# Seven products instead of eight in two FFNs, with three of the four sums of weights made by accumulating transfers

## The chip, the core and the metric

The kernel runs on one core of a Trainium2 chip. The metric is the device time of one execution in microseconds, as the median of several runs. The core's engines are TensorE (PE in the profile, with its weight loads as PEld), VectorE (DVE), ScalarE (ACT), GpSimd (POOL) and SyncE (SP); the last two issue transfers here, which 16 DMA engines carry out. Each engine works off its own instructions strictly in order, and so do the queues on which SyncE and GpSimd issue transfers: an instruction that waits holds up all that stand behind it.

## The reference

One block over 256 tokens of width 2048, all in float32. The change touches the two feed-forward networks (FFNs), whose hidden width is 5632:

```python
def swiglu_ffn(x, w_gate, w_up, w_down):
    return (jax.nn.silu(x @ w_gate) * (x @ w_up)) @ w_down
...
x = x + 0.5 * swiglu_ffn(rmsnorm(x, norm_ffn1_g[l]), ffn1_w_gate[l], ffn1_w_up[l], ffn1_w_down[l])
h = rmsnorm(x, norm_mix_g[l])
proj = h @ w_in[l]
... # attention in chunks and retention, each with its own output projection, merged by gates
x = x + merged @ w_out[l]
x = x + 0.5 * swiglu_ffn(rmsnorm(x, norm_ffn2_g[l]), ffn2_w_gate[l], ffn2_w_up[l], ffn2_w_down[l])
return rmsnorm(x, norm_final_g)
```

Gate and up are matrices of 2048 x 5632, down is one of 5632 x 2048. Between the two FFNs stand the mixers: an input projection 2048 x 11264 (`w_in`) and three output projections.

## The kernel before

**Steps.** All weights are streamed once, in blocks of 256 rows by 512 columns (512 KB, `KC` = 2 slices of 128 rows). One such block is a step, and the program is 768 steps in a row, 264 in each FFN and 240 in the mixers. A step loads its block on SyncE's queue into one of 4 raw buffers (L94; `raw` with a number in the rows). ScalarE then copies it to the reduced float32 type that TensorE reads at full rate (`hi`, L107), and VectorE subtracts that from the raw block to get what is left (`lo`, L108). There are 5 pairs of hi and lo buffers. I call this pair of operations a split. It is done a few steps ahead of use (`split_upto`), as far as the buffers go.

**Products.** The activations are split in the same way, once, when they are transposed. Each product is made of three, hi by hi, hi by lo and lo by hi (L125 to L127). The 256 tokens are two tiles of 128, so that a step has 2 slices x 2 token tiles x 3 = 12 matmuls of 128x128 by 128x512, with the weights moving. They add into two PSUM banks, one for each token tile (`acc`); there are four of those, and four more for transposes and the like (`side`).

**FFN.** The hidden columns are cut into 11 blocks of 512. A block has 8 steps of gate, after which ScalarE evicts the two banks with SiLU (L374), and 8 of up, after which VectorE multiplies (L379). Two steps later the product is transposed (L269) and split, as an operand of the down projection. Down runs in two halves, after blocks 0 to 5 and after blocks 6 to 10, and each half adds to the residual in SBUF (`xall`), with 4 x 12 or 4 x 10 steps. The norm's gain is put on in the transposes of the input (`put`, L322), its scale for each token at the evictions.

**Order.** A scheduler does not decide anything: the order on each engine is that of the program, with `later(n, fn)` to put work n steps on. At the start, loads of weights and the four column quarters of x are issued by turns (`load_x`, L173). The mixers use two tables of 512 KB each, which GpSimd's queue loads (`decay`, L201, and `biasT`, the bias read from the spread-out table `rel_ext`). The last `TAIL` = 4 steps are done token tile by token tile, so that the first one's finish overlaps the second one's products.

## Time and profile before

| what | value |
|---|---|
| median of 3 runs | 2179.64 us (2179.56 to 2180.44) |
| the profiled execution, its time and its span | 2180.46 us, 2178.4 us |
| TensorE clock granted, mean | 0.999 |
| busy: PE, PEld, DVE, ACT, POOL | 2167.7, 1802.5, 1121.6, 963.0, 21.6 us |
| moved by DMA | 414.51 MB, 190 GB/s in the mean |
| share of the 16 DMA engines taken by SyncE's queue (q1) | 57.9% |
| the chain that ended last | PE 99% |

The span goes from the first instruction to the last, and the time of an execution holds a little more than its span. In the rows below, a row of the waits or of the groups names engine, operation, output and inputs and line. In rows of the chain and of the timeline the first number is the time since the start of the span and the second the time until the last of the row's instructions ended, both in us; x4 is the number of instructions in the row; what stands in brackets is an idle time before it and what ended it. Rows of transfers give the size and the us from issue to landing. Busy time of an engine is an average over the whole span; what a wait costs is seen only at its own place.

### The profile page before, as it was taken

To read this page: it belongs to the slowest core of one execution; us is meant where nothing else is said; L and a number is where in the kernel's file an instruction comes from. 1 tells how busy PE (TensorE), PEld (TensorE's weight loads), DVE (VectorE), ACT (ScalarE), POOL (GpSimd) and SP (SyncE) were. 2 spreads that over 40 slices of the span, in tenths; PEclk is the share of its full clock that TensorE was granted. 3 is DMA by queue.
4 is the path that set the end of the run, shared out by engine and by line. 5 is a ranking of instruction groups with operands and counts; after the bars stand their busy time and mean duration, and the time that the engine had idled before them with its cause. 6 is when DMAs were issued, how large, how long until landed. Compare 5 with 4: busy or idle time off the path is not lost.

```text
span 2178.4 us, 25308 instructions
## 1 busy us (share of the span) xinstructions
PE 2167.7 (100%) x9865; PEld 1802.5 (83%) x9865; DVE 1121.6 (51%) x1192; ACT 963.0 (44%) x1104; POOL 21.6 (1%) x36
## 2 busy tenths in 40 slices
PE   9999999999999999999999999999999999999998
PEld 7888888888888888888888888888888888888887
DVE  5544554445545544556655555554544544444554
ACT  6444433444444444454444444454444433444443
POOL 0000000000000000000000000000000000000000
PEclk9999999999999999999999999999999999999999
DMA  7655655666665555555555555556656556666554
GB/s 253 208 188 187 222 192 194 212 188 190 187 209 184 184 190 187 175 163 178 167 177 190 188 192 192 185 183 194 193 184 193 189 194 212 189 192 191 186 192 137
DMA packets 213512, 414.51 MB, mean 190 GB/s; under 512 B 12864, under 2 KB 13616, under 8 KB 213392
## 3 DMA queue, kind: packets, MB, share of 16 engines
q1 hardware_dynamic: 211424, 406.90, 57.9%
q0 software_dynamic: 1824, 5.93, 0.9%
q8 instruction: 77, 1.26, 0.2%
q14 instruction: 43, 0.35, 0.0%
q10 hardware_dynamic: 144, 0.07, 0.0%
HBM read 409.17 MB, written 3.67 MB: 190 GB/s over the span
## 4 chain that ended last, share of the span: by engine, by line
PE 99%; issue 0%; DMA 0%; ACT 0%; DVE 0%; POOL 0%; POOLq 0%; ACTq 0%
PE acc L125 32%; PE acc L126 32%; PE acc L127 32%; PE f2a0p L269 0%; PE f1a0p L269 0%; PE n1p L322 0%; DMA grows<-in_norm_ffn_g_dram 0%; PE f2a6p L269 0%; PE f1a6p L269 0%; PE mgp L269 0%; PE nmp L322 0%; PE n2p L322 0%; PE as L479 0%; PE rs L537 0%; PE av L514 0%
## 5 line engine op out<-in xcount | busy, mean ns | idle before, releaser
L108 DVE TENSOR_TENSOR lo<-raw,hi 128x1024 fp32r<-128x1024 f32 (+1 forms) x769 | 938.8, 1223 | 1014.0 <-ACT hi L107 1013.6
L107 ACT CAST hi<-raw 128x1024 fp32r<-128x1024 f32 (+1 forms) x769 | 808.2, 1052 | 1106.8 <-PE acc L127 1081.8
L125 PE MATMUL acc<-hi,nmh 128*128 128x512 f32 x704 | 277.8, 395 | 0.0
L125 PE MATMUL acc<-hi,n1h 128*128 128x512 f32 x704 | 276.2, 392 | 0.0
L125 PE MATMUL acc<-hi,n2h 128*128 128x512 f32 x704 | 274.8, 390 | 0.0
L126 PE MATMUL acc<-lo,n1h 128*128 128x512 f32 x704 | 274.7, 390 | 0.0
L127 PE MATMUL acc<-hi,n1l 128*128 128x512 f32 x704 | 274.6, 390 | 0.0
L127 PE MATMUL acc<-hi,nml 128*128 128x512 f32 x704 | 274.5, 390 | 0.0
L126 PE MATMUL acc<-lo,nmh 128*128 128x512 f32 x704 | 274.1, 389 | 0.0
L127 PE MATMUL acc<-hi,n2l 128*128 128x512 f32 x704 | 274.0, 389 | 0.0
L126 PE MATMUL acc<-lo,n2h 128*128 128x512 f32 x704 | 273.9, 389 | 0.0
L127 PEld LDWEIGHTS acc<-hi,n1l 128*128 128x128 f32 x704 | 132.4, 188 | 27.6
L127 PEld LDWEIGHTS acc<-hi,nml 128*128 128x128 f32 x704 | 132.2, 188 | 27.9
L125 PEld LDWEIGHTS acc<-hi,n1h 128*128 128x128 f32 x704 | 132.6, 188 | 27.3
L126 PEld LDWEIGHTS acc<-lo,n1h 128*128 128x128 f32 x704 | 132.4, 188 | 27.3 <-DVE lo L108 0.4
L127 PEld LDWEIGHTS acc<-hi,n2l 128*128 128x128 f32 x704 | 132.2, 188 | 27.5
L126 PEld LDWEIGHTS acc<-lo,n2h 128*128 128x128 f32 x704 | 132.2, 188 | 27.1
L125 PEld LDWEIGHTS acc<-hi,n2h 128*128 128x128 f32 x704 | 132.2, 188 | 27.0
L126 PEld LDWEIGHTS acc<-lo,nmh 128*128 128x128 f32 x704 | 132.3, 188 | 26.2
L125 PEld LDWEIGHTS acc<-hi,nmh 128*128 128x128 f32 x704 | 132.3, 188 | 26.2
L125 PE MATMUL acc<-hi,f2a0h 128*128 128x512 f32 x192 | 74.8, 390 | 0.0
L125 PE MATMUL acc<-hi,f1a0h 128*128 128x512 f32 x192 | 74.8, 389 | 0.0
(266 smaller groups left out, 2107.3 us busy)
## 6 DMA issues: line engine op xcount, KB each, us to landing
raw<-in_ffn_w_up_dram SPq DMA_DIRECT2D x176, 512.0 KB, 3.5
raw<-in_ffn_w_down_dram SPq DMA_DIRECT2D x176, 512.0 KB, 3.6
raw<-in_w_in_dram SPq DMA_DIRECT2D x176, 512.0 KB, 3.5
raw<-in_ffn_w_gate_dram SPq DMA_DIRECT2D x175, 512.0 KB, 3.5
raw<-in_w_out_dram SPq DMA_DIRECT2D x32, 512.0 KB, 3.7
raw<-in_w_out_att_dram SPq DMA_DIRECT2D x16, 512.0 KB, 4.3
raw<-in_w_out_ret_dram SPq DMA_DIRECT2D x16, 512.0 KB, 4.3
xall<-in_x_dram SPq DMA_DIRECT2D x3, 512.0 KB, 7.5
```

The source lines that it names most:

```text
L107: nc.scalar.copy(hi[:, p, :], raw[:, p, :])
L108: nc.vector.tensor_sub(lo[:, p, :], raw[:, p, :], hi[:, p, :].bitcast(F32))
L125: nc.tensor.matmul(acc, ahi[:, ts], whi[:, cs], start=first, stop=False)
L126: nc.tensor.matmul(acc, ahi[:, ts], wlo[:, cs], start=False, stop=False)
L127: nc.tensor.matmul(acc, alo[:, ts], whi[:, cs], start=False, stop=last)
```

## The change

In each FFN, blocks 1 to 10 compute gate and up together; block 0 and all the down steps stay as they were. Take the activations X (256 tokens by 2048) as 2 x 2 parts: token halves 1 and 2 by two halves of the inner dimension, which alternate by four slices of 128. Take the weights of one block as 2 x 2 parts: the same two inner halves (top and bottom) by gate and up. Eight products of such parts give the result; the program now forms it from seven (a form of Strassen's scheme, due to Winograd), with sums of activations, sums of weights and sums of results.

The four sums of activations (s5, s7, s6, s3) are made once for each of the two FFN norms, by VectorE (`add_up`), and split like the rest. Four sums of weights are made for each block, 4 tiles of 512 KB each. Two sets of tiles stay in SBUF over the block: k, which begins as the top of gate, and x, which begins as the top of up.

- T1: x = x + k, an accumulating transfer from SBUF to SBUF on GpSimd's queue, issued when x's load is issued (`load_second`, L478 in the rows)
- T2: x = x + bottom of up, the same kind, up to 3 steps ahead of its use (`early`)
- T3: k = x - k, on VectorE (L517)
- T4: x = x + bottom of gate, an accumulating transfer again (L519)

So a block pair (I call it a group; there are 20) has these steps, each with a tile number 0 to 3:

| step | splits | products, bank |
|---|---|---|
| p0 to p3 (phase 0) | k, x (after T1) | X11 by k in a; s5 by x in c |
| q0 to q3 (phase 1) | bottom of up (raw), x (after T2) | s6 by x in a; s3 by raw in c |
| r0 to r3 (phase 2) | bottom of gate (raw), k (after T3) | s7 by k in a; X12 by raw in b |
| s0 to s3 (phase 3) | x (after T4) | X22 by x in a |

A step p, q or r has two splits and 12 matmuls (two products over one token half each), a step s has one split and 6. After each phase banks are evicted (`end`): after p3 ScalarE copies a and c; after q3 it copies a, and VectorE adds c to that; after r3 VectorE adds a and b to earlier results; after s3 ScalarE evicts a. SiLU and the multiplication follow as the parts come ready.

The group's steps are woven with 8 standard steps, D1 to D8, mostly of down, in this order: p0 p1 p2 p3 D1, q0 q1 D2 q2 q3 D3, r0 D4 r1 D5 r2 D6 r3 D7, s0 s1 s2 s3 D8 (`WOVEN`; the last group of an FFN has more of them). Down is no longer done in halves, but for each pair of blocks. The hi and lo buffers go from 5 pairs to 4, raw buffers stay at 4, 8 tiles (`KEPT`) hold k and x. A step is prepared only when as many split buffers are free as it needs, and while a step is prepared the transfers that have a buffer free are issued. In numbers of instructions: 9156 matmuls of 512 columns become 8724, 120 of 256 columns become 24; 769 casts become 1009; GpSimd issues 240 transfers more; SyncE issues 782 before and after.

```diff
-SPLIT_BUFS = 5
-ACT_TILES = 26
-TAIL = 4
+SPLIT_BUFS = 4
+KEPT = 8
+ACT_TILES = 30
+TAIL = 2
 AHEAD = (2, 3)
+BY_DMA = ("T1", "T2", "T4")
+HALF_K = D // P // 2
+LEAD = 8
+EARLY = 3
+WOVEN = "ppppD" "ppDppD" "pDpDpDpD" "ssssD"
+WOVEN_LAST = "pDppDpD" "pDpDpDpD" "pDpDpDpD" "ssDssD"
...
+    def load_some():
+        while state["dma"] < len(transfers):
+            ring, fn = transfers[state["dma"]]
+            if not room[ring]:
+                return
+            room[ring] -= 1
+            fn()
+            state["dma"] += 1
+
+    def prep_upto(n, c):
+
+        while state["prep"] < min(len(steps), n):
+            s = steps[state["prep"]]
+            if s.slots > state["slots"]:
+                return
+            load_some()
+            for e in steps[state["prep"] : state["prep"] + EARLY]:
+                if e.early is not None and e.early():
+                    e.early = None
+            state["slots"] -= s.slots
+            s.prep()
+            for ring in s.frees:
+                room[ring] += 1
+            state["prep"] += 1
+            load_some()
...
+        def add_up(self, p, n):
+
+            if n == 0:
+                self.f = [act_tile(F32, f"{self.name}f{p}{i}") for i in range(2)]
+                self.f = [f.rearrange("p a (h q) -> p h a q", h=2)[:, i] for f in self.f for i in range(2)]
+                x0, x1 = self.raw.pop(2 * p), self.raw.pop(2 * p + 1)
+                a11, a21, a12, a22 = [x[:, :, t * P : (t + 1) * P] for x in (x0, x1) for t in range(NT)]
+                s5, s7, s6, s3 = self.f
+                nc.vector.tensor_sub(s5, a22, a21)
+                nc.vector.tensor_sub(s7, a11, a21)
+                nc.vector.scalar_tensor_tensor(s6, s5, -1.0, a11, op0=ALU.mult, op1=ALU.subtract)
+                nc.vector.scalar_tensor_tensor(s3, s6, -1.0, a12, op0=ALU.mult, op1=ALU.subtract)
+            for i in (2 * n, 2 * n + 1):
+                self.split_to(self.SUMS[i], slice(4 * p, 4 * p + 4), self.f[i])
...
+            def load_second():
+                self.x[jc] = kept_tile("x")
+                fetch(self.x[jc], self.w[1], self.rows(0, jc), self.col[1])
+                if "T1" in BY_DMA:
+                    nc.gpsimd.dma_start(self.x[jc], self.kept[jc], accum_op=ALU.add)
+
+            def load_raw():
+                made["raw"] = weights_tile(f"raw{name}")
+                i = 2 - phase
+                fetch(made["raw"], self.w[i], self.rows(1, jc), self.col[i])
+
+            def early():
+
+                if "raw" not in made:
+                    return False
+                nc.gpsimd.dma_start(self.x[jc], made["raw"], accum_op=ALU.add)
+                return True
+
+            def two(first, second):
+
+                tiles = []
+                for i, raw in enumerate((first, second)):
+                    hi = wpool.tile([P, KC, NB], F32R, tag="hi", bufs=SPLIT_BUFS, name=f"hi{name}{i}")
+                    lo = wpool.tile([P, KC, NB], F32R, tag="lo", bufs=SPLIT_BUFS, name=f"lo{name}{i}")
+                    nc.scalar.copy(hi, raw)
+                    tiles.append((raw, hi, lo))
+                for raw, hi, lo in tiles:
+                    nc.vector.tensor_sub(lo, raw, hi.bitcast(F32))
+                return [(hi, lo) for _, hi, lo in tiles]
+
+            def prep():
+                x = self.x[jc]
+                if phase == 0:
+                    if "T1" not in BY_DMA:
+                        nc.vector.tensor_add(x, x, self.kept[jc])
+                    made["w"] = two(self.kept[jc], x)
+                elif phase == 1:
+                    raw = made["raw"]
+                    if "T2" not in BY_DMA:
+                        nc.vector.tensor_add(x, x, raw)
+                    made["w"] = two(raw, x)
+                elif phase == 2:
+                    raw, k = made.pop("raw"), self.kept.pop(jc)
+                    nc.vector.tensor_sub(k, x, k)
+                    if "T4" in BY_DMA:
+                        nc.gpsimd.dma_start(x, raw, accum_op=ALU.add)
+                    else:
+                        nc.vector.tensor_add(x, x, raw)
+                    made["w"] = two(raw, k)
+                else:
+                    made["w"] = [split(self.x.pop(jc), name)]
+
+            def products():
+                w = made["w"]
+                if phase == 0:
+                    self.product("a", "a00", jc, w[0], True, False)
+                    self.product("c", "s5", jc, w[1], True, False)
+                elif phase == 1:
+                    self.product("a", "s6", jc, w[1], False, False)
+                    self.product("c", "s3", jc, w[0], False, True)
+                elif phase == 2:
+                    self.product("a", "s7", jc, w[1], False, False)
+                    self.product("b", "a01", jc, w[0], True, True)
+                else:
+                    self.product("a", "a11", jc, w[0], False, True)
+                if jc == n - 1:
+                    self.end(phase)
...
+        def end(self, phase):
+
+            norm, acc, copy = self.norm, self.acc, self.copy
+
+            def copied(key, bank, scale):
+                copy[key] = tmp_tile(f"{self.name}{key}", "qk", 4)
+                nc.scalar.activation(copy[key], acc[bank], AF.Copy, scale=scale)
+
+            if phase == 0:
+                copied("s1", "a", norm.scale(0))
+                copied("s5", "c", norm.minus_scale(1))
+            elif phase == 1:
+                copied("s2", "a", norm.minus_scale(0))
+                r = copy["s2"]
+                nc.vector.scalar_tensor_tensor(r, acc["c"], norm.minus_scale(0), r, op0=ALU.mult, op1=ALU.add)
+                self.evict(0, 1, r)
+            elif phase == 2:
+                r = copy["s5"]
+                nc.vector.scalar_tensor_tensor(r, acc["a"], norm.minus_scale(1), r, op0=ALU.mult, op1=ALU.add)
+                self.evict(1, 1, r)
+                r = copy["s1"]
+                nc.vector.scalar_tensor_tensor(r, acc["b"], norm.scale(0), r, op0=ALU.mult, op1=ALU.add)
+                self.evict(0, 0, r)
+            else:
+                self.evict(1, 0, None, acc["a"])
...
+        queue = plain(0)
+        for pair in range((nblocks + 1) // 2):
+            queue += down(pair)
+        queue = [(job, k) for job in queue for k in range(0, job.nk, KC)]
+
+        def next_standard(n):
+            for job, k in queue[:n]:
+                steps.append(standard(job, k))
+            del queue[:n]
+
+        next_standard(LEAD)
+        for b in range(1, nblocks):
+            group = paired(b).steps()
+            for what in WOVEN if b < nblocks - 1 else WOVEN_LAST:
+                if what == "D":
+                    next_standard(1)
+                else:
+                    steps.append(group.pop(0))
+            assert not group
+        next_standard(len(queue))
```

On ScalarE, around the first eviction of a group, before: the casts of three steps, the two evictions of a gate block, and the casts of the next steps.

```order
L107 CAST hi41_978<-raw41_894 128x1024
L107 CAST hi42_996<-raw42_928 128x1024
L107 CAST hi43_1014<-raw43_946 128x1024
L374 ACTIVATE f1g20_1032<-acc32_0_876,n1rstd_88 128x512
L374 ACTIVATE f1g21_1034<-acc32_1_877,n1rstd_88 128x512
L107 CAST hi44_1036<-raw44_964 128x1024
L107 CAST hi45_1058<-raw45_982 128x1024
```

The same place after the change, the seam of phases 0 and 1 of a group whose first step is number 104 (z104; the two digits behind the name are phase and tile, the last is the first or second split of the step):

```order
L498 CAST hiz104030_2602<-z104k3_2461 128x1024
L498 CAST hiz104031_2605<-z104x3_2479 128x1024
L114 CAST hi108_2623<-raw108_2482 128x1024
L553 ACTIVATE z104s1_2641<-z104a_2567,n1rstd_88 128x512
L553 ACTIVATE z104s5_2643<-z104c_2574,n1minus_89 128x512
L498 CAST hiz104100_2645<-rawz10410_2484 128x1024
L498 CAST hiz104101_2648<-z104x0_2364 128x1024
```

Before, the casts of steps 41 to 43 stood ahead of the evictions after step 39's products; now one cast, that of D1, lies between p3's casts and the evictions, and q0's two come behind them. On VectorE at the seam of phases 1 and 2, after the change (before, the whole program had no such step):

```order
L501 TENSOR_TENSOR loz104131_2737<-z104x3_2479,hiz104131_2736 128x1024
L115 TENSOR_TENSOR lo114_2756<-raw114_2678,hi114_2755 128x1024
L561 SCALAR_TENSOR_TENSOR z104s2_2773<-z104c_2574,n1minus_89,z104s2_2773 128x512
L517 TENSOR_TENSOR z104k0_2362<-z104x0_2364,z104k0_2362 128x1024
L501 TENSOR_TENSOR loz104200_2779<-rawz10420_2697,hiz104200_2778 128x1024
L501 TENSOR_TENSOR loz104201_2782<-z104k0_2362,hiz104201_2781 128x1024
L115 TENSOR_TENSOR lo116_2789<-raw116_2719,hi116_2788 128x1024
```

The sum T3 for r0 (L517) and r0's two subtractions stand behind the addition from bank c, which needs q3's last product. On GpSimd, where the last sums of one group meet the first of the next (z128; before, this queue issued 21 transfers in all, none of them here):

```order
L519 DMA z104x1_2409<-rawz10421_2741 128x1024
L519 DMA z104x2_2454<-rawz10422_2786 128x1024
L478 DMA z128x0_2877<-z128k0_2875 128x1024
L519 DMA z104x3_2479<-rawz10423_2829 128x1024
L478 DMA z128x1_2922<-z128k1_2880 128x1024
L478 DMA z128x2_2967<-z128k2_2945 128x1024
```

The last T4 of the group (into x3, used by s3) now stands behind the first T1 of the next group. On SyncE at the start, before:

```order
L94 DMA raw6_177<-in_ffn1_w_gate_dram 128x2x512
L94 DMA raw7_206<-in_ffn1_w_gate_dram 128x2x512
L173 DMA xall_77<-in_x_dram 128x2x512
L94 DMA raw8_234<-in_ffn1_w_up_dram 128x2x512
L94 DMA raw9_240<-in_ffn1_w_up_dram 128x2x512
```

and after, up to the same loads:

```order
L108 DMA raw7_221<-in_ffn1_w_gate_dram 128x2x512
L108 DMA z8k0_223<-in_ffn1_w_gate_dram 128x2x512
L108 DMA z8x0_225<-in_ffn1_w_up_dram 128x2x512
L108 DMA z8k1_228<-in_ffn1_w_gate_dram 128x2x512
L108 DMA z8x1_230<-in_ffn1_w_up_dram 128x2x512
L108 DMA z8k2_233<-in_ffn1_w_gate_dram 128x2x512
L108 DMA z8x2_235<-in_ffn1_w_up_dram 128x2x512
L108 DMA z8k3_238<-in_ffn1_w_gate_dram 128x2x512
L108 DMA z8x3_240<-in_ffn1_w_up_dram 128x2x512
L219 DMA xall_77<-in_x_dram 128x2x512
L108 DMA raw12_271<-in_ffn1_w_up_dram 128x2x512
```

The eight loads of the first group's k and x, which have buffers from the beginning, now stand ahead of the last quarter of x.

More of the change, by code (lines that the diff above doesn't have):

```diff
@@ L150, in run @@
[L150 removed]
+            steps[c].products()
+            state["slots"] += steps[c].slots
+        prep_upto(len(steps), head)
         state["step"] = head
```

332 lines of the change are left out of this document (212 added, 120 removed).

## The prediction

> **What bounds the kernel now.** I read the page's head first, then the waits of TensorE, then the chain in order of time for the pace of a step.
>
> ```profile
> span 2178.4 us, 25308 instructions
> PE 2167.7 (100%) x9865; PEld 1802.5 (83%) x9865; DVE 1121.6 (51%) x1192; ACT 963.0 (44%) x1104; POOL 21.6 (1%) x36
> ...
> PE gps L184 <- DMA grows<-in_norm_ffn_g_dram: 1.8, 1, 1.8
> PE psw L685 <- POOL mhalf L206: 1.1, 1, 1.1
> ...
> 149.53 0.87 PE f1a0p L269 x8
> 193.94 0.87 PE f1a0p L269 x8
> ```
>
> TensorE is busy in all of the span, and its whole list of waits is 2.9 us. So a matmul less is its time less, as long as nothing new makes TensorE wait. From one set of transposes to the next lie 16 steps of 12 matmuls and 0.87 us of transposes: (193.94 - 149.53 - 0.87) / 192 = 0.2268 us a matmul, 2.72 us a step. One pair of weight blocks with its 8 standard steps ("a group") now costs 24 x 2.72 + 0.9 = 66.2 us.
>
> The other engines have room, and these are their paces when work stands in a row, and the handovers:
>
> ```profile
> 37.69 2.95 ACT L107 CAST hi<-raw 128x1024 fp32r<-128x1024 f32 x3
> 38.77 4.63 DVE L108 TENSOR_TENSOR lo<-raw,hi 128x1024 fp32r<-128x1024 f32 x4 [3.15 <-ACT hi L107]
> ...
> 563.89 1.05 ACT L107 CAST hi<-raw 128x1024 fp32r<-128x1024 f32 x1 [1.67 <-PE acc L127]
> 564.98 1.22 DVE L108 TENSOR_TENSOR lo<-raw,hi 128x1024 fp32r<-128x1024 f32 x1 [1.49 <-ACT hi L107]
> 565.51 0.39 PE L127 MATMUL acc<-hi,n1l 128*128 128x512 f32 x1
> 565.93 1.37 ACT L374 ACTIVATE f1g<-acc,n1rstd 128x512 f32<-128x512 f32 x2 [0.99 <-PE acc L127]
> 567.20 1.04 ACT L107 CAST hi<-raw 128x1024 fp32r<-128x1024 f32 x1
> ...
> L379 DVE SCALAR_TENSOR_TENSOR f1g<-acc,n1rstd,f1g 128x512 f32<-128x512 f32 x22 | 15.4, 743 | 0.0
> ```
>
> A cast takes 1.05 us, and one follows the next after 0.95; a subtraction takes 1.22 and follows after (4.63 - 1.23) / 3 = 1.13; it starts 0.04 after its cast ends (564.98 against 563.89 + 1.05). ScalarE reads a bank 0.42 us after its last matmul began, which is 0.19 after the next may start; two evictions take 567.20 - 565.93 = 1.27, so 0.64 each. An eviction on VectorE costs 15.4 / 22 = 0.70.
>
> **The change, part by part.** *Fewer products.* 20 groups each lose 192 - 168 = 24 matmuls: 480 x 0.2268 = **-108.9 us**, if TensorE goes on without a wait. Transposes stay the same. A group is then 264 x 0.2268 + 0.9 = 60.8 us.
>
> *More splits.* A group has 36 casts instead of 24 and 40 subtractions (36 splits, 4 of the sum left on VectorE). VectorE: 40 x 1.13 + 11 evictions and the like x 0.70 = 53 us of 60.8; ScalarE: 36 x 0.95 + 7 x 0.64 = 39 us. Neither becomes the bound on average, and I cost them nothing there. If the cover were gone, it would show at the seams between the phases, where a split can't be made ahead:
>
> *Seam of phases 0 and 1.* With four split buffers, step q0 is prepared only after p3 is issued, so on ScalarE its casts stand behind the two evictions that wait for p3. From p3's end: second eviction at 0.19, cast of the raw block at 0.83, cast of x 1.78 to 2.83; on VectorE lo of raw from 1.92, lo of x 3.05 to 4.27. TensorE has only D1 (2.72 us) to do, and its second matmul of q0, at 2.95, needs that lo: it waits 1.3 us.
>
> *Seam of phases 1 and 2.* VectorE evicts bank c at 0.19, then makes k (0.89 to 2.11), ScalarE casts k until 3.20, and lo of k ends at 4.46; cover again is one step, D3. Wait 1.5 us. The seam of phases 2 and 3 has D7 and s0 as cover and a chain of about the same length: nothing. Together 2.8 x 20 = **+57 us**; ends 0 (if a split is made earlier than I read) and 4 x 20 = 80 (if VectorE comes late to both).
>
> *The sums by transfer.* 12 a group, 512 KB each, 240 in all. No accumulating transfer is in this trace. The nearest rows are plain transfers of the same size on the same queue, two issued in a row, and what they did to the loads beside them:
>
> ```profile
> L201 POOL DMA_DIRECT2D decay<-in_decay_dram x2: 547/548/549, 616.5 to 617.1; - x2
> ...
> DMA to landing us min/median/max: 6.4/7.1/7.8
> ...
> DMA to landing us min/median/max: 5.6/6.1/6.6
> ...
> raw<-in_ffn_w_down_dram SPq DMA_DIRECT2D x176, 512.0 KB, 3.6
> ...
> raw<-in_ffn_w_down_dram SPq DMA_DIRECT2D x7, 512.0 KB, 4.5
> decay<-in_decay_dram POOLq DMA_DIRECT2D x2, 512.0 KB, 7.1
> ...
> raw<-in_ffn_w_gate_dram SPq DMA_DIRECT2D x4, 512.0 KB, 5.4
> ...
> 10.00:12.00 2.00, 2.00 (x6) 1.52 (x6) 2.00 (x4) 0.74 (x1) 0.00 (x0) 1.00 1.06 404
> ```
>
> The first two rows of landings are decay (6.4 and 7.8) and biasT (5.6 and 6.6). A load lands after 3.6 us alone (median of the run), 4.5 beside the decay pair and 5.4 beside the four of rel_ext. With all engines taken (share 1.06) they move 404 GB/s, so one pass over 512 KB is 1.30 us. The bounds for an accumulating one: 3.6 (a load alone) from below; from above, a second pass for itself and for the one in front of it (2.6), at half the rate where loads share the engines (5.2). I take the same-queue rows and half a second pass, since these are the same queue and shape.
>
> The Trainium skill (DMA: Bandwidth & Descriptors, "Anatomy of one DMA — SWDGE (gpsimd) path") gives 2.0 us plus the bytes at 436 GB/s for a transfer of this queue: 3.2 us for 512 KB. The trace's 5.6 to 7.8 beside loads disagrees; by the skill the two terms below would be nothing and the sum rival A's.
>
> *The last T4 of a group.* It stands on the GpSimd queue behind the first T1 of the next group, and that waits for loads. Clock from the end of r3: s3 starts at 2.72 + 3 x 1.36 = 6.8, its second matmul needs lo at 7.03, so the cast must begin, and T4 have landed, by 7.03 - 1.22 - 0.04 - 1.05 = 4.7. The load of x0 stands on SP's queue behind that of D8, which gets its buffer when lo of D6 ends. k of r2 can be cast when r1 has let its buffer go (-10.88 + 0.19), so lo of k ends at -8.4, lo of D6 at -7.2, later with the standard evictions between; I take -7. An issue on SP costs 0.47 us (row of the start, below). So x0 is issued at -6.1, lands 5.4 later at -0.7, T1 takes 0.55 to issue (decay's row), and T4 starts at -0.1. As decay's second (7.8) it lands at 7.7, 3.0 late; with a full second pass 5.6 late; sharing, 8.2. I take 4.3: **+86 us** for 20 groups, ends 0 and 164. Behind the waiting cast stand D8's and the next group's p0's, so nothing fills the gap.
>
> *T2 of q3.* Its raw block's buffer comes from q0, whose lo of raw ends at 3.14 after p3; load 4.5, T2 6.4: landed at 14.0. q3 starts at 14.9 (q0 to q2 and D2, with the wait above), and x must be cast by 12.9. Late 1.2: **+24 us**, ends 0 and 2.5 x 20 = 50. The other sums have about 1 us or more to spare by the same reckoning.
>
> *The start.*
>
> ```profile
> 3.21 0.47 SPq L173 DMA_DIRECT2D xall<-in_x_dram  x1
> ...
> 10.18 7.18 SPq L94 DMA_DIRECT2D raw<-in_ffn_w_gate_dram  x4
> 17.40 0.46 SPq L173 DMA_DIRECT2D xall<-in_x_dram  x1
> ...
> xall<-in_x_dram SPq DMA_DIRECT2D x1, 512.0 KB, 5.5
> ...
> 22.66 0.58 PEld L322 LDWEIGHTS n1p<-id_sb,xall 128*128 128x128 f32 x4
> ```
>
> The last quarter of x is issued at 17.40, lands at 22.9 and is used as it lands. Now eight loads of k and x go ahead of it: 3.8 us of issuing to 10.4 us of data (8 x 1.30). I take **+8.5**. The sums of activations, once a norm, fall where VectorE is half idle: 0.
>
> *The end.* TAIL goes from 4 to 2, so the second half's last products follow the first half's 2.7 us sooner, and its finish queues behind the first's: **+1.5** (0 to 2.6).
>
> **Sum**: 2178.4 - 108.9 + 57 + 86 + 24 + 8.5 + 1.5 = 2246.5 us of span. The profiled execution took 2180.46 for its 2178.4, 0.8 above the median of the three runs, so 1.2 goes on top: **2248 us**, 3% slower.
>
> **Rivals.** *A: the sums are ready in time, and it is faster.* If the last T4 lands within 4.8 us of issue, only the seams remain: 2178.4 - 108.9 + 57 + 8.5 + 1.5 + 1.2 = 2138 us. For it: the data goes from SBUF to SBUF, and 3.6 us is what a load takes. Against: the rows of that queue. It decides at a lateness of (108.9 - 57 - 10) / 20 = 2.1 us a group: below that the kernel gains. *B: the DMA engines become the bound*, because a sum reads two operands: a group then needs 24 x 1.30 + 12 x 2.60 = 62.4 us of all 16 engines at their best, with 63.6 to do it in, and the loads of eight blocks, two T4 and four T1 all fall about the s steps. Everything then lands at its upper bound, 8.2 and 2.5 late: 2138 + 214 = 2352 us. For it: 404 GB/s was the most that slices showed. Against: an average under 1 still fits. The Trainium skill (Collectives: The Full Stack, "The bandwidth ceiling: the fold count and why AG ≠ RS ≠ AR") says that adding in the transfer is not slow by itself, but reads two sources through the same ring and so halves the rate (62.28 against 32.35 GB/s); no run here shows it yet. *C: the waits just eat the gain*, lateness 2.1 us: 2180 us. That the change does nothing is excluded: the matmuls are not in the program.
>
> **How the numbers follow.** The forecast 45% (its own range 2195 to 2300), A 27%, B 23%, C 5%. A measurement of this kernel tells about 0.2% from no change. Faster is A, 0.27; same is C, 0.05; slower the rest, 0.68. The range reaches from just under A, where the seams are shorter, to B: 2128 to 2350.
>
> **What would show it.** Right: TensorE busy below 97% in the FFNs and 100% between them; waits of matmuls for lo and hi of z blocks, and of casts of x for transfers; the last T4 landing 7 us or more after issue; a group 69 to 71 us long; the transposes of x's last quarter near 31 us. B: DMA share near 1.0 through the FFNs. A: landings of 3.6 to 5 us and groups of 64 us. I would be wrong in the seams if q0 and r0 start on time.

## The result and the profile after

The changed kernel takes 2489.06 us (median of 4 runs, 2478.95 to 2495.95), the one before 2179.6 beside it: a ratio of 1.1415, with an interval of 1.1375 to 1.1455. It is 14% slower, where 3% was forecast, and lies outside the range (2128 to 2350). The page's head, in its first rows:

```profile
span 2488.6 us, 26066 instructions
PE 2188.5 (88%) x9337; PEld 1753.2 (70%) x9337; DVE 1568.6 (63%) x1670; ACT 1245.3 (50%) x1468; POOL 228.2 (9%) x276
...
PEclk8989898989899999999999999999898989989999
...
q1 hardware_dynamic: 211424, 406.90, 50.1%
q0 software_dynamic: 36384, 131.77, 27.1%
...
raw<-in_ffn_w_down_dram SPq DMA_DIRECT2D x176, 512.0 KB, 6.3
```

Two things are to be seen. TensorE is idle for 300 us (2488.6 - 2188.5), where it was idle for 10.7. And it is busy for 20.8 us longer than before with 528 rows fewer, although 108.9 us of products are gone: the clock row has dropped in both FFNs. So 129.7 us are matmuls that took longer. On the engines' side, q0, the GpSimd queue, takes 27.1% of the 16 DMA engines where it took 0.9%: (0.271 x 2488.6 - 19.6) / 240 = 2.73 us of all engines for each sum. A load takes 0.501 x 2488.6 / 776 = 1.61 us, and lands after 6.3 us, not 3.6.

TensorE's waits by what released them (total, times, longest), for the longest of all and for the group whose first step is 104:

```profile
PE n1p L386 <- DMA xall<-in_x_dram: 16.2, 1, 16.2
...
PE z104a L122 <- ACT hiz L114: 7.4, 1, 7.4
...
PE z104a L122 <- ACT hiz L498: 3.6, 2, 3.2
...
PE z104a L123 <- DVE loz L501: 2.2, 3, 0.9
```

L114 is the cast of a block used alone, which for a z tile is an s step. Added up over the 20 groups, the waits for the s steps are 152.1 us, those for casts of other z blocks 59.7, those for their lo parts 51.3. The chain of waits of the group's end, in order of time (start, duration, what):

```profile
441.95 6.28 DMA z128k<-in_ffn_w_gate_dram
...
448.27 1.61 issue
449.88 0.02 POOLq L519
449.90 0.09 POOL z128x L478
449.99 0.49 issue
450.48 11.70 DMA z104x<-rawz
...
462.28 1.05 ACT hiz L114
463.33 0.02 issue
463.36 1.24 DVE loz L115
464.59 0.04 issue
464.64 0.80 PE z104a L123
465.44 0.43 PE z104a L124
```

It reads as forecast: the last T4 (450.48) stands on the queue behind the next group's first T1 (449.90), which stood there until its x had been loaded, and s3's cast starts as the T4 has landed. What was not forecast is its 11.7 us, and the last row: the matmuls behind the wait come at 0.43 us instead of 0.227. The same in stretches of 5 us, with the busy times of PE, PEld, DVE, ACT and POOL, the granted clock, the engines' share and GB/s:

```profile
410.00:415.00 5.00, 5.00 (x24) 4.13 (x22) 2.36 (x2) 1.75 (x2) 0.86 (x1) 1.00 1.03 310
415.00:420.00 5.00, 1.32 (x4) 0.44 (x2) 1.43 (x2) 1.99 (x2) 0.00 (x0) 0.81 0.44 102
420.00:425.00 5.00, 5.00 (x12) 3.95 (x13) 0.93 (x1) 1.62 (x2) 0.00 (x0) 0.51 0.43 143
...
455.00:460.00 5.00, 0.96 (x5) 0.46 (x3) 0.00 (x0) 0.00 (x0) 0.86 (x1) 0.91 1.08 248
460.00:465.00 5.00, 1.16 (x2) 0.65 (x3) 1.64 (x2) 2.72 (x3) 0.00 (x0) 0.50 1.05 245
465.00:470.00 5.00, 5.00 (x14) 3.94 (x14) 3.60 (x4) 2.79 (x4) 0.28 (x1) 0.57 1.04 333
470.00:475.00 5.00, 5.00 (x28) 4.22 (x27) 4.69 (x6) 3.47 (x5) 2.17 (x3) 1.00 1.07 291
```

Behind the waits of 3.2 and 7.4 us TensorE is "busy" for 5 us with 12 and 14 matmuls instead of 24, at a clock of 0.5 to 0.6. While it waits for s3, the DMA engines are full (1.05 to 1.08).

### The profile page after: what moved, and what is told of

It reads as the page before. It is cut to its first block, busy times and chain, and to the rows that moved or that the text cites. A ratio compares the mean times of both kernels' runs of the same rounds, so it can differ in the third digit from the quotient of the medians.

```text
span 2488.6 us, 26066 instructions
## 1 busy us (share of the span) xinstructions
PE 2188.5 (88%) x9337; PEld 1753.2 (70%) x9337; DVE 1568.6 (63%) x1670; ACT 1245.3 (50%) x1468; POOL 228.2 (9%) x276
## 3 DMA queue, kind: packets, MB, share of 16 engines
q0 software_dynamic: 36384, 131.77, 27.1%
## 4 chain that ended last, share of the span: by engine, by line
PE 50%; DMA 32%; DVE 6%; ACT 5%; issue 4%; SPq 0%; POOL 0%; ACTq 0%; POOLq 0%; DVEq 0%
PE acc L122 11%; PE acc L123 11%; PE acc L124 11%; DMA raw<-in_ffn_w_down_dram 4%; DMA rawz<-in_ffn_w_up_dram 4%; DVE loz L501 2%; ACT hiz L498 2%; DVE loz L115 1%; DMA z608x<-rawz 1%; DMA z8x<-rawz 1%; DMA z680x<-rawz 1%; DMA z152x<-rawz 1%; DMA z200x<-rawz 1%; DMA z584x<-rawz 1%; DMA z704x<-rawz 1%
## 5 line engine op out<-in xcount | busy, mean ns | idle before, releaser
L115 DVE TENSOR_TENSOR lo<-raw,hi 128x1024 fp32r<-128x1024 f32 (+1 forms) x449 | 546.2, 1221 | 360.0 <-ACT hi L114 357.5
L114 ACT CAST hi<-raw 128x1024 fp32r<-128x1024 f32 (+1 forms) x449 | 469.7, 1048 | 405.7 <-PE acc L124 320.2
L501 DVE TENSOR_TENSOR loz<-rawz,hiz 128x1024 fp32r<-128x1024 f32 x160 | 195.2, 1220 | 76.9 <-ACT hiz L498 74.6
L498 ACT CAST hiz<-rawz 128x1024 fp32r<-128x1024 f32 x160 | 167.5, 1047 | 54.5 <-PE acc L124 24.8
L122 PE MATMUL acc<-hi,nma00h 128*128 128x512 f32 x176 | 70.6, 401 | 0.0
L122 PE MATMUL acc<-hi,nma01h 128*128 128x512 f32 x176 | 70.1, 398 | 0.0
L124 PE MATMUL acc<-hi,nma00l 128*128 128x512 f32 x176 | 68.7, 390 | 0.0
L124 PE MATMUL acc<-hi,nma01l 128*128 128x512 f32 x176 | 68.6, 390 | 0.0
L122 PE MATMUL acc<-hi,nma10h 128*128 128x512 f32 x176 | 68.6, 390 | 0.0
L123 PE MATMUL acc<-lo,nma00h 128*128 128x512 f32 x176 | 68.6, 390 | 0.0
L123 PE MATMUL acc<-lo,nma11h 128*128 128x512 f32 x176 | 68.5, 389 | 0.0
L123 PE MATMUL acc<-lo,nma10h 128*128 128x512 f32 x176 | 68.5, 389 | 0.0
```

Of the source, the lines that this page charges most:

```text
L114: nc.scalar.copy(hi[:, p, :], raw[:, p, :])
L115: nc.vector.tensor_sub(lo[:, p, :], raw[:, p, :], hi[:, p, :].bitcast(F32))
L122: nc.tensor.matmul(acc, ahi, whi, start=first, stop=False, **more)
L123: nc.tensor.matmul(acc, ahi, wlo, start=False, stop=False, **more)
L124: nc.tensor.matmul(acc, alo, whi, start=False, stop=last, **more)
L498: nc.scalar.copy(hi, raw)
```

## The experiments

All are edits of the changed kernel. Seven groups of the first FFN, from the eviction after phase 0 of its second group to that of the ninth, give the time of a group: (724.5 - 155.7) / 7 = 81.3 us in the changed kernel, 60.8 if TensorE never waited.

| run | what differs | us | ratio to before (interval) | group, us |
|---|---|---|---|---|
| changed | | 2489 | 1.1415 (1.1375 to 1.1455) | 81.3 |
| e1 | no T1, T2, T4 | 2166 | 0.994 (0.992 to 0.996) | 64.7 |
| e10 | as e1, start and seams mended | 2111 | 0.969 (0.967 to 0.971) | 61.7 |
| e8 | T4 alone | 2191 | 1.006 (1.004 to 1.008) | 65.9 |
| e16 | T1 alone | 2231 | 1.024 (1.021 to 1.027) | 68.3 |
| e3 | order on the queue | 2409 | 1.105 (1.103 to 1.106) | 77.7 |
| e4 | as e3, start | 2394 | 1.099 (1.097 to 1.101) | 77.7 |
| e13 | as e4, loads spread | 2368 | 1.087 (1.083 to 1.090) | 75.8 |
| e9 | as e4, small down loads | 2309 | 1.060 (1.057 to 1.063) | 72.7 |
| e17 | as e4, plain copies | 2224 | 1.021 (1.014 to 1.027) | 68.4 |
| e2 | plain copies | 2347 | 1.077 (1.074 to 1.079) | 74.2 |
| e7 | waits filled | 2472 | 1.134 (1.132 to 1.137) | 79.6 |
| e5 | all sums on VectorE | 2303 | 1.057 (1.055 to 1.059) | 71.7 |
| e6 | as e4, sums on GpSimd itself | 2558 | 1.174 (1.172 to 1.176) | 86.1 |
| e15 | T4 by transfer, rest VectorE | 2303 | 1.057 (1.053 to 1.060) | 71.7 |
| e11 | as e15, other order | 2322 | 1.065 (1.063 to 1.067) | 72.7 |
| e14 | T2, T4 by transfer | 2352 | 1.079 (1.076 to 1.082) | 73.7 |
| e12 | T1, T4 by transfer | 2404 | 1.103 (1.101 to 1.105) | 78.1 |

**What the sums cost, and what is left without them (e1, e10).**

```diff
-                if "T1" in BY_DMA:
-                    nc.gpsimd.dma_start(self.x[jc], self.kept[jc], accum_op=ALU.add)
...
-                nc.gpsimd.dma_start(self.x[jc], made["raw"], accum_op=ALU.add)
...
-                    if "T4" in BY_DMA:
-                        nc.gpsimd.dma_start(x, raw, accum_op=ALU.add)
-                    else:
-                        nc.vector.tensor_add(x, x, raw)
```

> All 240 sums by transfer are left out (x is used as it was loaded; T3 on VectorE stays), so nothing waits for the GpSimd queue and its transfers take nothing from the DMA engines. Theory S (the weave itself is too tight: two splits made after an eviction): most of the lost time stays, over 2350 us, and q3 and s3 still start late. Theory D (the sums by transfer are late): s3 and q3 start on time, only the seams at q0 and r0 (some 2.5 us a group, 50 in all) and the late last quarter of x (16) are left: 2178.4 - 108.9 + 50 + 16 + 2 = about 2138 us, groups of 63 us, TensorE's clock back above 0.98.

e10 leaves out the same, issues the last quarter of x right behind the third, lets ScalarE copy bank c between q0's two casts (`put_off`), and turns the order of the two splits in q and of the two products in r:

```diff
-                    made["w"] = two(raw, x)
+                    made["w"] = two(x, raw, self.put_off.pop() if jc == 0 else None)[::-1]
...
+                    self.product("b", "a01", jc, w[0], True, True)
                     self.product("a", "s7", jc, w[1], False, False)
-                    self.product("b", "a01", jc, w[0], True, True)
...
     load_x(2 * NB, 3 * NB)
+    load_x(3 * NB, 4 * NB)
```

> As e1_no_sums (no sums T1, T2, T4 at all), with the last quarter of x early, and the two seams taken apart: in q steps x is split ahead of raw (its product comes first) and ScalarE copies bank c between q0's two casts; in r steps the product of raw comes ahead of that of k, which has to wait for T3. Theory S (the 4.5 us by which a group without sums is above 60.8 are the seams at q0 and r0, 1.42 and 1.76 us with what the restart costs): some 2.6 us a group go, and 8.8 at the start: 2095 to 2125 us. Rival (ScalarE and VectorE are late there by their amount of work, so that the wait moves to the second product or the next step): 2140 us or more.

Measured 2166 and 2111: e1 is the case of theory D, 28 us above its estimate, and e10 that of theory S. So the sums cost 323 us, and this order of steps would gain only 13 us if they were free: a group is still 64.7 - 60.8 = 3.9 us too long, 78 us in 20 groups. In e1's timeline, TensorE's waits within a group, the first at q0 and two at r0:

```profile
330.80 0.50 PE L123 MATMUL z104a<-loz,n1s6h 128*128 128x512 f32 x1 [0.95 <-DVE loz L498]
...
347.65 0.50 PE L122 MATMUL z104a<-hiz,n1s7h 128*128 128x512 f32 x1 [0.47 <-ACT hiz L495]
...
348.92 0.49 PE L123 MATMUL z104a<-loz,n1s7h 128*128 128x512 f32 x1 [0.76 <-DVE loz L498]
```

These are the places of the forecast, at 2.2 us of wait. From start to start of a matmul these three take 1.45, 0.85 and 1.27 us instead of 0.23, and three beside them 0.33, so that they cost 3.2 us. Another order of the same work takes most of it away: e10's page has

```profile
span 2109.1 us, 25320 instructions
PE 2077.8 (99%) x9337; PEld 1708.4 (81%) x9337; DVE 1568.2 (74%) x1670; ACT 1247.5 (59%) x1468; POOL 21.6 (1%) x36
```

That is 3.1% below the kernel before, and the room within which the sums would have to stay: 68.5 us, 3.4 a group.

**The place on the queue (e3, e4).**

In e3 a T1 of the next group is kept back (`hold`) until the last T4 is issued. e4 does that too, and issues the last quarter of x right behind the third, as e10 does.

```diff
+                if hold["on"]:
+                    hold["t1"].append(t1)
+                else:
+                    t1()
...
+                    nc.gpsimd.dma_start(x, raw, accum_op=ALU.add)
+                    hold["on"] = jc < n - 1
+                    while not hold["on"] and hold["t1"]:
+                        hold["t1"].pop(0)()
```

> Only the order on GpSimd's queue changes: the first T1s of the next group stand behind the last T4 of this one. Theory Q (the place on the queue): the last T4 is issued when its block and k are there, about 443 instead of 450.5 us in the group of step 104, lands in 5 to 7 us, s3 starts on time, and the slow clock behind that wait goes too: (7.6 + 2.4) x 20 = 200 us less, about 2290 us. Theory E (the DMA engines are full): a group needs 24 x 1.61 + 12 x 2.73 = 71.4 us of all 16 engines, of 81.7 now; the T4 then takes 9 us or more to land, the wait moves to the first T1 or to T2, and the time stays above 2380 us.

> As e3_order, and the last quarter of x is issued right behind the third, ahead of the first group's eight loads of k and x. The transposes waited 16.2 us for that quarter; with it early they should wait 2 us or less, and the time should be 12 to 16 us below e3_order. If the start is bound by the transfers in any order, the wait only moves to the first blocks of weights: less than 4 us below.

Measured 2409 and 2394. The start is 14 us, as expected. The order is 80, not 200: theory E. The wait for s3 was gone, and another stood in its place, on ScalarE at the cast of p0's x (start, duration, line, in brackets the wait):

```profile
431.95 1.04 ACT L504 CAST hiz<-z128x 128x1024 fp32r<-128x1024 f32 x1 [6.24 <-DMA z128x<-z128k]
432.90 0.68 ACT L639 ACTIVATE f1h<-z104a,n1rstd 128x512 f32<-128x512 f32 x1
```

Behind that cast on ScalarE stands the last eviction of the group, then VectorE's multiplication, and so TensorE waits at the transposes (in e4: "f1a1p <- DVE f1h", 9.1 us in 2). The T4 had moved in front of the T1, and the T1 came late instead. Its new place on the queue was not what held it: in this group x0's load was issued at 412.23 us and landed 10.5 us later (7.3 in the changed kernel), T1 was issued at once, at 422.77, and landed after another 9.2 us, while the last T4 beside them took 10.0.

**The engines' work, or the way from load to cast (e2, e9, e17).** In e2 and e17 the three `accum_op=ALU.add` are left out, in e17 on top of e4. In e9, also on top of e4, for the down steps alone (`small`):

```diff
+            if small:
+                r0 = job.row0 + k0 * P
+                nc.sync.dma_start(made["raw"][:, 0, : NB // 2], job.w[r0 : r0 + P, job.col0 : job.col0 + NB // 2])
+                return
...
+                src = raw[:, 0:1, : NB // 2].to_broadcast([P, 2 * KC, NB // 2])
```

> The same 240 transfers on the same queue at the same places, but as plain copies without adding (the sums are then wrong; times alone are read). If what hurts is the accumulation (2.73 us of all 16 DMA engines each, by 27.1% of 2488.6 us less 19.6 over 240, against 1.61 for a load, by 50.1% of 2488.6 over 776): the share of the GpSimd queue falls from 27% to about 16%, the last T4 lands in 6 us instead of 11.7, and the time falls to 2250 to 2330 us. If it is the place on the queue (T4 of tile 3 behind the next group's first T1, issued 8 us after its operands are there): the last T4 still starts 8 us late, s3 still waits 3 us or more, 2350 to 2430 us.

> The kernel of e4_order_start with all its 240 sums by transfer as they are, but each down step in the FFNs loads only a quarter of its block (128 KB) and uses it four times, so that casts, subtractions and matmuls stay the same and only the loads beside the sums get smaller. Theory E (the DMA engines are the bound): a group needs 16 x 1.61 + 8 x 0.40 + 12 x 2.73 = 61.7 us of them instead of 71.4; the time falls by 110 to 175 us from 2394, to 2220 to 2285 us. Theory L (a sum by transfer takes too long by itself): the sums land as late as before, and the time stays above 2365 us.

> The kernel of e4_order_start (2394 us) with its 240 sums as plain copies (the sums are then wrong; times alone are read): the same queue, places and bytes written, and a share of the DMA engines of 1.36 instead of 2.73 us each (14.8% of 2340.1 less 19.6, over 240, in e2_plain). Theory A (the engines' work sets the pace once the order is right): a group needs 38.6 + 12 x 1.36 = 54.9 us of them instead of 71.4 and is bound by TensorE and the seams again: 2180 to 2250 us. Theory L (each sum's way from load to cast is too long, whatever the engines' work): over 2320 us.

Measured 2347, 2309 and 2224. In e2 both causes stand together, and the result lies between the two ranges. e9 falls between the theories: 85 us. e17 decides, since it differs from e4 only in that a transfer neither reads its destination nor adds to it: 170 us less, within theory A's range. The GpSimd queue's row, of e4 and then of e17:

```profile
q0 software_dynamic: 36384, 131.77, 28.6%
```

```profile
q0 software_dynamic: 36384, 131.77, 15.5%
```

The same packets and bytes, and 2.77 against 1.36 us of all engines for each ((0.286 x 2392.2 - 19.6) / 240 and (0.155 x 2228.0 - 19.6) / 240): accumulating doubles a transfer's work on the engines. No run here parts the second read from the addition. The doubling is what the Trainium skill (Collectives: The Full Stack, "The bandwidth ceiling: the fold count and why AG ≠ RS ≠ AR") says of adding on the way, that two sources share the rate, and here the trace agrees with a factor of 2.04. What is left from e17 to a group without sums (68.4 against 64.7) was not taken apart: the way through a transfer is still longer than none, and the copies still take 16 us of the engines a group.

**The crowd at the end of a group (e8, e13, e16).** e8 keeps T4 alone, e16 T1 alone. e13 changes e4's order of loads; the first four keys are the places of k0, x0, k1 and x1:

```diff
+            keys = [at[id(d[4])] + 0.1, at[id(d[5])] + 0.1, at[id(d[6])] + 0.1, d1 + 0.1] + late
...
+    transfers.extend(ld for _, _, ld in sorted(keyed, key=lambda e: e[:2]))
```

> Only the T4 sums stay, by transfer as in the changed kernel; T1 and T2 are left out (x is used as loaded). 4 of 12 transfers a group. Theory E (the DMA engines are full): a group takes 38.6 + 4 x 2.73 = 49.5 us of them, far from full, so a T4 lands in about 5 us and s3 starts on time: 2166 to 2185 us, the time without sums. Theory L (a sum by transfer is too slow by itself, whatever lies beside it): s3 still waits 3 us or more, 2250 us or more; the lone T4s would explain their third of the 323 us.

> The changed kernel with T1 alone by transfer, T2 and T4 left out: as e8_t4_alone, where four sums a group cost 25 us over the kernel without sums (2166). Theory A (the average use of the engines, 49.5 us of 65 in both): about the same, 2170 to 2210 us. Theory B (T1 falls into the crowd of eight loads and has to land before p0): 2230 us or more, and the wait stands at p0 to p3.

> The kernel of e4_order_start with the next group's eight loads of k and x spread over phases 2 and 3 (k0 behind D5's load, x0 behind D6's, k1 behind D7's, x1 behind the next D1's, the rest behind the next q1's) instead of all behind D8's. The sums and the bytes stay the same. Theory A (the DMA engines are full on average): a group needs 71.4 us of them whatever the order; its 77.6 us can fall by a few at most, 2330 us or more. Theory B (the crowd at the end of a group): T1 is ready when p0 is due, the waits at p0 to p3 and at the transposes behind them go (some 8 us a group with the slow clock), 2230 to 2290 us, with the sums' share of the engines as before.

Measured 2191 (6 us above theory E's range), 2231 (theory B) and 2368 (theory A). Four sums a group cost 25 us where they are T4s: three of the four are issued ahead of the crowd of loads (in the group of step 104 of e8 at 351.4, 356.0 and 361.9 us, the fourth at 367.0; the eight loads go from 365.8 to 373.4 us). They cost 65 us where they are T1s, all four behind those loads and due at the very start of the next group (7 of the 65 at the start, where x's last quarter waits longer). So the place counts as long as the engines have room. With all twelve it counts little: spreading gave 26 us. The row of the seven groups (us, busy PE, PEld, DVE, ACT, POOL, clock, engines' share, GB/s), of the changed kernel, of e13 and of e1:

```profile
155.70:724.50 568.80, 472.58 (x1907) 369.42 (x1907) 377.80 (x362) 282.97 (x302) 80.25 (x95) 0.91 0.88 238
```

```profile
133.90:664.20 530.30, 469.80 (x1906) 359.62 (x1904) 376.87 (x362) 280.37 (x302) 80.63 (x95) 0.96 0.94 255
```

```profile
128.60:581.60 453.00, 435.55 (x1906) 352.58 (x1905) 377.37 (x362) 284.38 (x301) 5.80 (x8) 1.00 0.62 201
```

0.88 x 568.8 / 7 = 71.5 and 0.94 x 530.3 / 7 = 71.2: a group takes 71 us of all 16 engines in either order, which agrees with 24 x 1.61 + 12 x 2.73 = 71.4 (40.1 without the sums). The price of a sum hardly depends on the crowd: by the queue's share it is 2.85 us in e8 (11.3% of 2188.4) and 2.60 in e16 (10.2% of 2229.9). TensorE needs 60.8. So an order of these transfers that kept the engines busy all the time would still take 71 us a group, about (71.2 - 66.2) x 20 = 100 us more than the kernel before. e13 comes to 75.8. The same row reads 0.87 in e9, that is 63.2 of its 72.7 us: there the engines had room on average, and whether the crowd or the length of each sum's way held the group was not taken apart.

**The clock (e7).**

```diff
+FILL = {1: 12, 3: 30}
...
+                if jc == n - 1 and phase in FILL:
+                    ps = side_tile(f"fill{name}")
+                    for _ in range(FILL[phase]):
+                        nc.tensor.matmul(ps[:, :P], id_sb, id_sb, start=True, stop=True)
```

> The changed kernel with work put into the two long waits: 12 small matmuls of the identity ahead of q3's products and 30 ahead of s3's (about 0.22 us each at full clock: 2.6 and 6.6 us, where TensorE waits 3.7 and 7.9 us); their result is not used. Theory C (a wait also costs the clock: 12 to 14 matmuls behind each take 0.427 instead of 0.227 us, 5.2 us a group, 104 in all): the wait stays as long, the matmuls behind it run at 0.23, and the time falls by 60 to 110 us to 2380 to 2430 us. Rival (what comes behind the wait is bound by transfers anyway, so that time won there is waited for later): 2470 us or more.

Measured 2472: 17 us less, at a clock of 0.984 instead of 0.943, which is the rival's range. Groups fell from 81.3 to 79.6 us in the first FFN and from 81.2 to 78.0 in the second, 1.7 to 3.2 of the 5.2 expected; in the last group of the first FFN, which hardly waited, the filling itself cost time, and a lead of 14.6 us shrank to 6.7. The slow clock is real, but with the engines full the time won on TensorE is in good part waited for again.

**Other places for the sums (e5, e6, e11, e12, e14, e15).** e5 sets `BY_DMA = ()`; e6 is e4 with `nc.gpsimd.tensor_add` for the three transfers; e11 and e12 are e10's order with `BY_DMA = ("T4",)` and `("T1", "T4")`; e14 and e15 are e13's loads with `("T2", "T4")` and `("T4",)`, x ahead of raw in q0 alone.

> All four sums of weights are made by VectorE, none by transfer; nothing else changes. It tells what the three sums by transfer are worth against the engine that they relieve. A group of the kernel without the sums took (651.1 - 128.6) / 8 = 65.3 us, with VectorE busy for about 53; 12 sums of 1.13 us more make 66.6 us of work, so VectorE becomes the bound. Theory D (the transfers are the dear way): still far below the changed kernel, with groups of 70 to 74 us: 2166 + 20 x (5 to 9) = 2260 to 2340 us. Theory V (VectorE would be dearer still, with each sum ahead of the splits that wait for it): over 2420 us.

> The order of e4_order_start, with T1, T2 and T4 as additions that the GpSimd engine itself computes instead of transfers. No row shows what such an addition takes. Theory E (the DMA engines are full of sums): the engines are left with 24 loads a group, 38.6 us; if an addition takes less than 3 us, the sums are ready and the time is that without sums less the start, 2150 to 2175 us, level with or below the kernel before. If it takes 5 us (60 us a group) GpSimd becomes the bound: 2250 us or more. If VectorE's subtractions get slower beside it (1.22 us now), as a rival: groups of 70 us or more with VectorE busy throughout.

> All sums are made. The order of e10_seams, T4 by transfer, T1 and T2 on VectorE. VectorE's work in a group is 53 + 8 x 1.13 = 62 us, that of the DMA engines 38.6 + 10.9 = 49.5 us. If VectorE can work nearly without a gap: groups of 64 us and 2140 to 2175 us, at or below the kernel before. Rival: the sums stand ahead of the splits that wait for them, as in e5_on_vector, where 12 sums cost 137 us: 8 of them 92, and T4's 25: 2105 + 117 = about 2220 us.

> As e11_t4_by_dma, with T1 by transfer too, behind the last T4 on the queue; T2 alone on VectorE. The DMA engines need 38.6 + 8 x 2.73 = 60.4 us of a group, VectorE 53 + 4.5 = 57.6. If the averages decide: 2130 to 2175 us, below e11. Theory E, sharper (what decides is the crowd at the end of a group, where eight loads of k and x, two T4 and four T1 fall together): T1 lands late as in e4_order_start, and the time is over 2210 us, above e11.

> All sums made: T2 and T4 by transfer, T1 on VectorE, the loads of k and x spread as in e13_spread, the last quarter of x early, the seams as in e10_seams (x ahead of raw in q0 alone). Work in a group: VectorE 53 + 4 x 1.13 = 57.6 us, DMA engines 38.6 + 8 x 2.73 = 60.4, TensorE 60.8. Theory B (places, not averages): 2140 to 2180 us, at or below the kernel before. Theory A: with two units full at 95% to 97%, any unevenness is a wait, over 2230 us.

> As e14, with T2 on VectorE too (only T4 by transfer): VectorE 53 + 8 x 1.13 = 62.1 us a group, the DMA engines 49.5. e11 (x ahead of raw in all q steps, loads not spread) took 2322. If e11 was slow since in its q steps the sum, the cast and the subtraction of x stood in a row with nothing beside them: 2200 to 2250 us here. If the sums on VectorE are late in any order: above 2300 us.

Measured, in this order, 2303, 2558, 2322, 2404, 2352 and 2303: e5 within theory D, e12 and e14 by the worse of their cases, e15 at the edge of it, and e11 100 us above even its rival. None is below the kernel before. VectorE is the cheaper place (e5 is 186 us below the changed kernel), and there it is the bound, busy for 471 of 502 us in the seven groups:

```profile
137.90:640.00 502.10, 448.79 (x1906) 347.25 (x1905) 470.73 (x447) 280.12 (x301) 5.79 (x8) 1.00 0.56 181
```

e12 is slower than e11 though VectorE has less to do (410 against 441 us in the seven groups) and the DMA engines are not full (0.77 against 0.69): T1 comes late as in e4, and TensorE waits at the same transposes (7.6 to 9.6 us in 2 for each of eight). In e15 VectorE is busy for 441 of 502 us, in e14 for 409 of 516 with the DMA engines at 0.81: neither unit is full on average, and yet the groups are 11 to 13 us too long. Which unevenness costs them most was not taken apart. e6 met its rival. Its rows on GpSimd and on VectorE, in the timeline about the s steps:

```profile
460.84 3.27 POOL L524 TENSOR_TENSOR z104x<-z104x,rawz 128x1024 f32<-128x1024 f32 x1 [3.49 <-issue]
464.89 2.55 POOL L479 TENSOR_TENSOR z128x<-z128x,z128k 128x1024 f32<-128x1024 f32 x1 [0.78 <-DMA z128x<-in_ffn_w_up_dram]
```

```profile
461.90 3.28 DVE L507 TENSOR_TENSOR loz<-z104k,hiz 128x1024 fp32r<-128x1024 f32 x1
465.11 3.40 DVE L116 TENSOR_TENSOR lo<-raw,hi 128x1024 fp32r<-128x1024 f32 x1
468.44 3.42 DVE L116 TENSOR_TENSOR loz<-z104x,hiz 128x1024 fp32r<-128x1024 f32 x1
```

An addition takes 2.4 to 3.4 us on GpSimd, and VectorE's subtraction beside it 3.3 to 3.4 instead of 1.22. The Trainium skill (SBUF — State Buffer, "Who interferes with whom") has this: a VectorE instruction with two inputs in SBUF and a GpSimd instruction that reads SBUF exclude each other. The trace agrees as far as these rows go: the first two subtractions end 1.07 us after the additions beside them (465.18 after 464.11, 468.51 after 467.44), about the 1.13 that one takes by itself.

## Why the prediction was wrong, point by point

The span grew by 310.2 us where 68.1 were forecast. The products gave their 108.9 us back; the waits of TensorE grew by 289.4 us (300.1 - 10.7) where 175.5 stood in the sum (and 1.5 for the end); and its matmuls took 129.7 us longer, where nothing stood. So two steps failed: the landing of the sums was read from rows of plain transfers, and a wait was given no price beyond its own length. That it is slower, and where TensorE waits, was forecast for reasons that the runs bear out. A group took 81.3 us where 69 to 71 were the sign to look for, and the transposes of x's last quarter came at 43 us, not near 31.

- **Fewer products, -108.9: held.** In e10, where the sums are gone and the seams mended, a group takes 61.7 us (forecast 60.8) and TensorE waits 19.4 us in all.
- **Seams, +57 (ends 0 and 80): the place held, the size was up to 78, by e1.** In the group shown the waits are 2.2 of 2.8 us; the late starts beside each wait were not in the sum. e10's order takes 60 of the 78 away ((64.7 - 61.7) x 20).
- **The last T4, +86 (ends 0 and 164): mis-sized.** The waits at the s steps are 152 us. x0 was issued 5.8 us ahead of r3's end (forecast 6.1) and landed after 7.3 us (forecast 5.4), the T4 was issued 0.58 after T1 (0.55), and it landed after 11.7 us where half a second pass was added to decay's 7.8 (9.1 in all). The step that failed is the choice of plain transfers' rows for it. They were too few to fill the engines; here eight loads, a T1 and a T4 of double work share them.
- **T2 of q3, +24 (ends 0 and 50): mis-sized.** Casts of z blocks outside the s steps held up TensorE for 59.7 us in all; in the group shown, 3.2 of 3.6 us are q3.
- **The start, +8.5: 16.2.** Its upper bound was near 10, since the T1s were not counted beside the eight loads: without them the wait is 8.8 (e1), with T1 alone 16.2 (e16). e4 got 14 back. The last quarter was issued 6.3 us later than before (23.67 against 17.40) and landed after 19.2 us instead of 5.5. The row at 22.66 that the forecast took for its first use belongs to the third quarter. The last one was first used at 25.84 before, 2.9 us after it had landed, and this room was not in the sum; after the change it was used at 43.01, as soon as it had landed.
- **The clock: nothing in the sum, 129.7 us longer busy.** This is the step that was missing; about 30 of them stand in e1 too (2088.7 against 2058.8), which has few long waits, and 19 in e10. The waits were added up as if TensorE went on at full pace behind them. What the slow clock is worth is less than its size, since e7 won only 17 us with most of it gone. The Trainium skill (TensorE: Matmul & The Clock Gate, "What's actually happening") says that an idle window of about 3.4 us halves the clock, and that it takes about as long of work to get it back. The trace agrees that the clock is halved behind the waits of 3.2 and 7.4 us (0.427 us a matmul), but it took 5 to 6 us of work to come back. Nor does it take one long window: in e16 waits of 1.69 and 0.76 us, with one matmul between them, were followed by eight matmuls at 0.425 us (clock 0.61). In e1, waits under 1 us left it at 1.00.
- **Rival B came nearest, and its bound had the right form.** Its 2352 us were still 137 short, and its sign, a DMA share near 1.0 through the FFNs, was met at the ends of groups (1.05 to 1.08) but is 0.88 over seven of them. It put a sum at 2.60 us of all engines and a load at 1.30, by the best rate of a slice (whose share was 1.06, which makes it 1.38); measured were 2.73 and 1.61, the average. By 62.4 us "an average under 1 still fits"; with 71.4 against 60.8 it does not. The load's average stood in the page that the prediction began from: 57.9% of 2178.4 us over 776 is 1.63.

## What to carry to other kernels

An accumulating transfer is to be counted as two passes on the DMA engines, and loads by their average share on the page, not by the best slice: bytes that look hidden at 58% are not when work of 2.7 us each joins them. Before the arithmetic of a scheme is trimmed, its bookkeeping (sums, splits, evictions) has to find an engine with room at that place; here TensorE gave up 5.4 us a group, and in none of the places tried did 12 sums cost less. A wait of 3 us on TensorE, or two shorter ones close together, cost the clock behind it as well, but removing a wait only helps as far as the next one allows.

## What the hardware did that was not expected

- Plain copies in the place of accumulating ones (e17), with the same packets and bytes, took the queue's work per transfer from 2.77 to 1.36 us and 170 us from the kernel.
- GpSimd's additions made VectorE's two-input subtractions 2.8 times as long (3.40 against 1.22 us), so moving the sums off VectorE cost both engines.
- A T4 beside the crowd took 11.7 us to land; the fastest in the same chain of waits took 4.54 us.
- Waits of 1.69 and 0.76 us close together were enough to halve TensorE's clock for 3 us (e16).
